# A macaron transformer block on one core: the mix stage's low-part subtractions in pieces of 256 columns, and a second factor of 1.0 in the bias scaling

## The chip, the cores and the metric

One core of one Trainium2 chip. The metric is device time in microseconds of one execution of the whole program; the kernel before takes 1156.02 us (median of 3 runs, 1155.96 to 1157.16).

## What is computed

The input `x` has 512 positions of 1024 features, in float32. One layer does, in this order:

```python
h = h + 0.5 * swiglu(rmsnorm(h, ffn1_norm), ffn1_w_gu, ffn1_w_down)      # 1024 -> 2 x 2816 -> 1024
u = rmsnorm(h, mix_norm)
qa, ka, va, qb, kb, vb, qi, ki, wi, g = split(u @ w_in)                  # 8 + 8 heads of 64, 4 index heads, 2 x 1024 gates
out_a = dsa_attention(...)     # per query the 128 keys with the best index scores
out_b = moba_attention(...)    # causal; own block of 256 and the block before
mixed = sigmoid(g_a) * (out_a @ w_branch_dsa) + sigmoid(g_b) * (out_b @ w_branch_moba)
h = h + mixed @ w_out
h = h + 0.5 * swiglu(rmsnorm(h, ffn2_norm), ffn2_w_gu, ffn2_w_down)
```

Both attentions add to their logits a bias looked up from the distance of query and key (`rel_bias`, 32 buckets, one column a head).

## The kernel before, in words

**Split products.** The matmuls take a reduced format (float32r). So that the result keeps float32's precision, every matrix is split into a high part (rounded to that format) and a low part (what rounding left), and a product is three matmuls: high by high, high by low, low by high. These are lines 118, 119 and 120, and they are most of what TensorE does.

**A weight unit.** Weights arrive in units of 128 x 1024 (some of 128 x 768 or 128 x 512) that serve one output tile. `wunit` (line 111) starts the DMA of a unit into `raw` (3 buffers) from SyncE's queue; `wsplit` (line 107) has ScalarE write the high part `whi` (line 108) and GpSimd the low part, `wlo = raw - whi` (line 109), with 3 buffers each. Ten units, late in the mix stage, and the first ones of the program have VectorE as the subtracting engine in place of GpSimd.

**Stages.** The first feed-forward block (`ffn`) takes until 380 us, the mix stage from there to 795 us, the second feed-forward block the rest. The mix stage first projects q, k and v of one head pair; then `weave` runs the MoBA attention (some 400 to 540 us) and fills TensorE's order with further projections, one step of three matmuls at a time; then come the branch products of MoBA, interleaved with gates, while VectorE finds the top 128 scores (540 to 600 us: `topk`, lines 530 to 534); then the DSA attention, woven in the same way (600 to 722 us); then the DSA branch and the output projection (to 795 us).

**One attention step.** For head and query block `i`, `logits(i)` puts the scores in PSUM (lines 587, 588), `addend(i + 1)` scales the next bias rows by the reciprocal of the query's norm, and line 596 (VectorE) adds the two and takes the row minimum; ScalarE exponentiates (line 75); `turn` transposes the probabilities on TensorE (line 623), and lines 631 and 632 split them into high and low. The scaling of the bias (`addend`, line 573) is GpSimd's in all 32 steps of MoBA and, in DSA, for the first query block of each head (40 instructions in all); the other DSA steps have it on VectorE together with the selection mask (line 570). GpSimd also multiplies each head pair's result by its reciprocal sums (line 652). The norms of q and k are small VectorE steps (lines 411 to 418, on 128 x 8) and some of 512 columns (445, 446, 453).

**Order.** TensorE's order is the program's, written by hand. The other engines' orders are set when the program is built, by a planner that plays the program through with its own costs for each instruction, and takes what is ready by priority (program order, with lines 596 and 75 of the attention raised). Each engine then runs its instructions strictly in that order.

Of the kernel before, what the change touches and what calls it, by code (L numbers as in the profile page):

```python
# [14 lines left out]
ALU = mybir.AluOpType  # L15
# [30 lines left out]
def f32(ap):  # L46
    return ap.bitcast(F32)
# [3 lines left out]
def block_kernel(ctx, tc, x, gains, wgu1, wd1, w_in, w_v, wb_a, wb_b, w_out, wgu2, wd2, rel_bias, onehot, out):  # L51
    nc = tc.nc
# [34 lines left out]
    def T(tag, bufs, shape=(P, S), dt=F32, p=sb):  # L87
        uid[0] += 1
        return p.tile(list(shape), dt, tag=tag, name=f"{tag}{uid[0]}", bufs=bufs)
# [4 lines left out]
    def mmps():  # L94
        return T("mm", 3, p=ps)
# [8 lines left out]
    def wtiles(n):  # L104
        return (T(t, b, (P, 1024), dt)[:, 0:n] for t, b, dt in (("raw", RAWS, F32), ("whi", 3, F32R), ("wlo", 3, F32R)))

    def wsplit(raw, hi, lo, eng=nc.gpsimd):
        nc.scalar.activation(hi, raw, AF.Copy)  # L108
        eng.tensor_sub(lo, raw, f32(hi))  # L109

    def wunit(src, eng=nc.gpsimd):
        raw, hi, lo = wtiles(src.shape[1])
        nc.sync.dma_start(raw, src)
        wsplit(raw, hi, lo, eng)
        return tuple(a.rearrange("p (k c) -> p k c", c=P) for a in (hi, lo))
# [10 lines left out]
    def together(gens):  # L126

        for _ in zip(*gens):
            pass
        for g in gens:  # L130
            run(g)

    def mmk(pt, w, xs):
        wh, wl = w
        n = wh.shape[1]
        for k in range(n):
            mm3(pt, wh[:, k, :], wl[:, k, :], xs[k][0], xs[k][1], k == 0, k == n - 1)
            yield
# [81 lines left out]
    def norm_r(ssum):  # L220
        p, ones = tps(), tmp()[:, 0:P]
        nc.gpsimd.memset(ones, 1.0 / D)
        nc.tensor.matmul(p, ones, ssum, start=True, stop=True)
        y, b = rsqrt_parts(p)
        r = T("R", 1)
        nc.vector.tensor_scalar(y, y, -0.5, None, op0=ALU.mult)
        nc.vector.scalar_tensor_tensor(r, b, -3.0, y, op0=ALU.add, op1=ALU.mult)
        return r
# [50 lines left out]
    def lead1(tiles, start, begun):  # L279

        ws = []
        for k in range(KD):
            nc.sync.dma_start(h[k], x[k * P:(k + 1) * P, :])
            if k % 2 == 0:
                pieces = [a.rearrange("p (k u c) -> p k u c", k=2, c=P) for a in wtiles(1024)]
            raw, hi, lo = (a[:, k % 2] for a in pieces)
            for i in range(2):
                nc.sync.dma_start(raw[:, 2 * i:2 * i + 2],
                                  wgu1[i * NF:i * NF + 2, :, k * P:(k + 1) * P].rearrange("u p c -> p u c"))
            ws.append((raw, hi, lo))  # L290
        pts = [f() for f in (mmps, mmps, sps, sps)]
        for k, (raw, hi, lo) in enumerate(ws):
            wsplit(raw, hi, lo, nc.vector)
            xs1.append(scaled(k, G_N1, h[k]))
            squares(k, ss1)
            if k == KD - 1:
                r = norm_r(ss1)
            for u, pt in enumerate(pts):
                mm3(pt, hi[:, u], lo[:, u], *xs1[k], k == 0, k == KD - 1)
        for u in (0, 2, 1, 3):  # L300
            tiles.append((pts[u], ()))
        begun[0] = 2
        start()
        return r
# [154 lines left out]
    def v_units(br, j, dsts, bank=mmps):  # L459


        vs = []

        def post(t, p):
            for e, v in enumerate(vs):
                src = p[:, e * P:(e + 1) * P].rearrange("p (e d) -> p e d", e=2)
                nc.scalar.activation(v[:, t, :, 0, :], src, AF.Copy, scale=r2T[:, t:t + 1])
                nc.vector.scalar_tensor_tensor(v[:, t, :, 1, :], src, r2T[:, t:t + 1], f32(v)[:, t, :, 0, :],
                                               op0=ALU.mult, op1=ALU.subtract)

        ws = [wunit(w_v[4 * br + 2 * j + i]) for i in range(2)]
        wh, wl = ([a.rearrange("p k c -> p (k c)").rearrange("p (k c) -> p k c", k=4)[:, k] for a in w for k in range(4)]
                  for w in zip(*ws))
        for t in range(NQ):
            if t % 2 == 0:
                p = bank()
            o = p[:, (t % 2) * 256:(t % 2 + 1) * 256]
            b = slice(t * P, (t + 1) * P)
            for k in range(KD):
                mm3(o, us[k][0][:, b], us[k][1][:, b], wh[k], wl[k], k == 0, k == KD - 1)  # L480
                if k % 2:
                    tick()
                    yield
            if t == 1:
                vs.extend(T("v", 3, (P, NQ, 2, 2, DH), F32R) for _ in dsts)
                for v, dst in zip(vs, dsts):
                    dst.append(v.rearrange("p t e s d -> p t e (s d)"))
            if t % 2:
                post(t - 1, p[:, 0:256])
                post(t, o)  # L490
# [58 lines left out]
    def attention(br, pairs, outs, extra):  # L549

        sel = br == 0
        bias, prob, tms, osum, tot, inv_s = {}, {}, {}, {}, {}, {}
# [5 lines left out]
        def rows(qt):  # L558
            return T(f"l{qt}", 1, (P, P * (qt + 1)))

        def addend(i):

            if i < 32:
                hd, qt = divmod(i, 4)
                W = P * (qt + 1)
                inv = pairs[hd // 2][0][2][:, 2 * qt + hd % 2:2 * qt + hd % 2 + 1]
                tms[i] = rows(qt)
                b = bias[hd][:, S - W:S]
                if sel and qt:
                    nc.vector.scalar_tensor_tensor(tms[i], b, inv, work[:, WOFF[qt]:WOFF[qt] + W],  # L570
                                                   op0=ALU.mult, op1=ALU.add)
                else:
                    nc.gpsimd.tensor_scalar(tms[i], b, inv, None, op0=ALU.mult)

        def logits(i):
            if i >= 32:
                return
            hd, qt = divmod(i, 4)
            if qt == 1:
                table(hd + 1)  # L580
            e = hd % 2
            (q, f, _), (k, kl), _ = pairs[hd // 2]
            W = P * (qt + 1)
            N = max(W, 256)
            p = sps()
            qb = q[:, e, qt * P:(qt + 1) * P]
            nc.tensor.matmul(p[:, 0:N], qb, k[:, e, 0:N], start=True, stop=False)
            nc.tensor.matmul(p[:, 0:N], qb, kl[:, e, 0:N], start=False, stop=True)
            addend(i + 1)
            pe = tms.pop(i)  # L590
            st = T("st", 8, (P, 4))
            if i % 8 == 0:
                tot[hd // 2] = T("tot", 2, (P, 8))
            s1 = tot[hd // 2][:, i % 8:i % 8 + 1]
            with tc.high_priority(HURRY):
                sums[i] = nc.vector.tensor_tensor_reduce(  # L596
                    out=pe, in0=p[:, 0:W], in1=pe, scale=f[:, 2 * qt + e:2 * qt + e + 1], scalar=3e38, op0=ALU.add, op1=ALU.min, accum_out=st[:, 0:1])
                log_exp(pe, pe, AF.Exp, bias=st[:, 0:1], scale=-1.0, accum_out=s1)
            prob[i] = pe
# [54 lines left out]

        table(0)
        addend(0)
        logits(0)
        yield 2
# [60 lines left out]
    def vv(br, j, **kw):  # L719
        return v_units(br, j, [a[2] for a in (dsa, moba)[br][2 * j:2 * j + 2]], **kw)  # L720

    ps3 = [mmps() for _ in range(2)]
    together([mmk(p, wunit(w_in[U_QB + 4 * i]), us) for i, p in enumerate(ps3)])
    v0 = vv(1, 0, bank=sps)
# [81 lines left out]
        run(unit(w_out[c], mixed, lambda p: wout_post(c, p)))  # L806


    def lead2(tiles, start, begun):
        start()  # L810
        together([t[1] for t in tiles])
        start()
        next(tiles[2][1])
        return norm_r(ss3)

    def emit(c, b):
        nc.sync.dma_start(out[c * P:(c + 1) * P, b], h[c][:, b])

    ffn(xs2, wgu2, wd2, emit, lead2, halves)


# [48 lines left out]
```

## Time and profile before

| | |
|---|---|
| median of 3 runs | 1156.02 us |
| profiled execution, its own time | 1157.22 us |
| its span, first to last instruction | 1155.4 us |
| granted TensorE clock, mean | 0.997 |
| TensorE busy (matmul) | 1137.6 us, 98% |
| VectorE busy | 670.6 us, 58% |
| ScalarE busy | 468.5 us, 41% |
| GpSimd busy | 529.5 us, 46% |

An engine's idle time ahead of an instruction is put down to what ended it. [...]

### The profile page before, as it was taken

To read this page: it belongs to the slowest core of one execution; us is meant where nothing else is said; L and a number is where in the kernel's file an instruction comes from. 1 tells how busy PE (TensorE), PEld (TensorE's weight loads), DVE (VectorE), ACT (ScalarE), POOL (GpSimd) and SP (SyncE) were. 2 spreads that over 40 slices of the span, in tenths; PEclk is the share of its full clock that TensorE was granted. 3 is DMA by queue.
4 is the path that set the end of the run, shared out by engine and by line. 5 is a ranking of instruction groups with operands and counts; after the bars stand their busy time and mean duration, and the time that the engine had idled before them with its cause. 6 is when DMAs were issued, how large, how long until landed. Compare 5 with 4: busy or idle time off the path is not lost.

```text
span 1155.4 us, 14050 instructions
## 1 busy us (share of the span) xinstructions
PE 1137.6 (98%) x5364; PEld 947.0 (82%) x5364; DVE 670.6 (58%) x966; ACT 468.5 (41%) x765; POOL 529.5 (46%) x283
## 2 busy tenths in 40 slices
PE   9999999999999999989999999999999999999998
PEld 7778888888888888779878877888888888888887
DVE  5864156613657468799967795764764156523551
ACT  6322123212234568758237766444322222322321
POOL 3444444444444656755454532044454444444442
PEclk9999999999999999989999999999999999999999
DMA  7233222332223221221242221322223322322322
GB/s 235 85 117 98 91 104 97 91 99 102 87 83 122 69 106 65 101 74 46 92 137 84 92 84 45 128 94 91 108 91 95 106 92 91 109 92 91 105 79 91
DMA packets 39580, 111.72 MB, mean 97 GB/s; under 512 B 4535, under 2 KB 9049, under 8 KB 39513
## 3 DMA queue, kind: packets, MB, share of 16 engines
q1 hardware_dynamic: 39368, 110.80, 29.0%
q8 instruction: 42, 0.69, 0.2%
q14 instruction: 26, 0.20, 0.1%
q10 hardware_dynamic: 144, 0.02, 0.0%
HBM read 108.64 MB, written 2.17 MB: 96 GB/s over the span
## 4 chain that ended last, share of the span: by engine, by line
PE 84%; DVE 7%; issue 4%; ACT 3%; POOL 1%; DMA 0%; SPq 0%; ACTq 0%; POOLq 0%; DVEq 0%
PE mm L120 20%; PE mm L118 20%; PE mm L119 20%; PE s L118 7%; PE s L119 7%; PE s L120 7%; DVE l L596 1%; POOL wlo L109 1%; ACT l L75 1%; PE pt L623 1%; DVE l L570 1%; DVE pt L632 1%; DVE a L146 1%; DVE fq L416 1%; POOL os L652 1%
## 5 line engine op out<-in xcount | busy, mean ns | idle before, releaser
L109 POOL TENSOR_TENSOR wlo<-raw,whi 128x1024 fp32r<-128x1024 f32 (+2 forms) x189 | 453.0, 2399 | 538.8 <-ACT whi L108 534.6
L108 ACT ACTIVATE whi<-raw 128x1024 fp32r<-128x1024 f32 (+2 forms) x207 | 205.1, 993 | 513.8 <-PE mm L119 299.0
L118 PE MATMUL mm<-x,whi 128*128 128x512 f32 x632 | 252.7, 400 | 0.5 <-ACT whi L108 0.5
L120 PE MATMUL mm<-x,wlo 128*128 128x512 f32 x632 | 247.4, 391 | 0.0
L119 PE MATMUL mm<-x,whi 128*128 128x512 f32 x632 | 247.0, 391 | 0.0
L118 PE MATMUL mm<-a,whi 128*128 128x512 f32 (+1 forms) x462 | 178.6, 387 | 1.3 <-DVE tmp L701 1.3
L120 PE MATMUL mm<-a,wlo 128*128 128x512 f32 (+1 forms) x462 | 178.6, 387 | 0.7 <-POOL wlo L109 0.7
L119 PE MATMUL mm<-a,whi 128*128 128x512 f32 (+1 forms) x462 | 178.7, 387 | 0.3
L120 PEld LDWEIGHTS mm<-x,wlo 128*128 128x128 f32 x632 | 118.9, 188 | 25.9 <-DVE wlo L109 0.3
L118 PEld LDWEIGHTS mm<-x,whi 128*128 128x128 f32 x632 | 119.4, 189 | 22.9 <-ACT whi L108 1.3
L118 PE MATMUL s<-x,whi 128*128 128x512 f32 x352 | 137.0, 389 | 0.6 <-ACT tmp L75 0.6
L120 PE MATMUL s<-x,wlo 128*128 128x512 f32 x352 | 137.0, 389 | 0.0
L119 PE MATMUL s<-x,whi 128*128 128x512 f32 x352 | 136.9, 389 | 0.0
L119 PEld LDWEIGHTS mm<-x,whi 128*128 128x128 f32 x632 | 119.2, 189 | 21.1 <-issue 0.5
L271 DVE SCALAR_TENSOR_TENSOR h<-mm,h 128x512 f32<-128x512 f32 (+1 forms) x49 | 33.3, 680 | 165.3 <-PE mm L120 165.3
L262 DVE TENSOR_TENSOR tmp<-tmp,tmp 128x512 f32<-128x512 f32 x44 | 99.0, 2250 | 29.3 <-ACT tmp L75 29.1
L146 DVE TENSOR_TENSOR a<-tmp,a 128x512 fp32r<-128x512 f32 x49 | 88.5, 1806 | 28.6 <-ACT a L145 28.3
L118 PEld LDWEIGHTS mm<-a,whi 128*128 128x128 f32 x462 | 86.8, 188 | 19.3 <-issue 1.7
L119 PEld LDWEIGHTS mm<-a,whi 128*128 128x128 f32 x462 | 86.8, 188 | 18.7 <-DVE a L146 1.1
L120 PEld LDWEIGHTS mm<-a,wlo 128*128 128x128 f32 x462 | 86.8, 188 | 18.6 <-POOL wlo L109 1.1
L118 PEld LDWEIGHTS s<-x,whi 128*128 128x128 f32 x352 | 66.1, 188 | 14.7 <-ACT tmp L75 1.0
L119 PEld LDWEIGHTS s<-x,whi 128*128 128x128 f32 x352 | 66.1, 188 | 13.8
(172 smaller groups left out, 1387.5 us busy)
## 6 DMA issues: line engine op xcount, KB each, us to landing
raw<-in_ffn_w_gu_dram SPq DMA_DIRECT2D x84, 512.0 KB, 3.4
raw<-in_w_in_dram SPq DMA_DIRECT2D x35, 512.0 KB, 3.5
raw<-in_ffn_w_down_dram SPq DMA_DIRECT2D x32, 512.0 KB, 3.5
raw<-in_ffn_w_down_dram SPq DMA_DIRECT2D x16, 384.0 KB, 3.1
bias<-fd SPq DMA_DIRECT2D x16, 256.0 KB, 3.5
raw<-in_w_v_dram SPq DMA_DIRECT2D x8, 512.0 KB, 3.4
raw<-in_w_out_dram SPq DMA_DIRECT2D x8, 512.0 KB, 3.5
h<-in_x_dram SPq DMA_DIRECT2D x8, 256.0 KB, 4.7
```

The lines of the kernel that those rows point to most:

```text
L75: op = after([group["load"]], lambda: nc.scalar.activation(*a, **k))
L108: nc.scalar.activation(hi, raw, AF.Copy)
L109: eng.tensor_sub(lo, raw, f32(hi))
L118: nc.tensor.matmul(pt, wh, xh, start=start, stop=False)
L119: nc.tensor.matmul(pt, wh, xl, start=False, stop=False)
L120: nc.tensor.matmul(pt, wl, xh, start=False, stop=stop)
L146: nc.vector.tensor_sub(lo, src, f32(hi))
L262: nc.vector.tensor_mul(g1, g1, s)
L271: nc.vector.scalar_tensor_tensor(h[c][:, b], pd, 0.5, h[c][:, b], op0=ALU.mult, op1=ALU.add)
L416: nc.vector.scalar_tensor_tensor(b, b, -3.0, y, op0=ALU.add, op1=ALU.mult)
L570: nc.vector.scalar_tensor_tensor(tms[i], b, inv, work[:, WOFF[qt]:WOFF[qt] + W], op0=ALU.mult, op1=ALU.add)
L596: sums[i] = nc.vector.tensor_tensor_reduce(out=pe, in0=p[:, 0:W], in1=pe, scale=f[:, 2 * qt + e:2 * qt + e + 1], scalar=3e38, op0=ALU.add, ...
```

## The change

`wsplit` gets a piece width. It is 1024 at first, so one instruction a unit as before; it is set to 256 ahead of the first projections of the mix stage and back to 1024 ahead of the second feed-forward block. In between, each subtraction on GpSimd goes in pieces of 256 columns: four for a unit of 1024 columns, two for one of 512. Subtractions on VectorE, and tiles of more than two dimensions, stay whole. In `addend`, GpSimd's multiplication of the bias by a per-row factor gets a second multiplication, by 1.0.

```diff
+    piece = [1024]
+
     def wsplit(raw, hi, lo, eng=nc.gpsimd):
         nc.scalar.activation(hi, raw, AF.Copy)
-        eng.tensor_sub(lo, raw, f32(hi))
+        if len(raw.shape) > 2 or eng is not nc.gpsimd:
+            eng.tensor_sub(lo, raw, f32(hi))
+            return
+        for c in range(0, raw.shape[1], piece[0]):
+            b = slice(c, min(c + piece[0], raw.shape[1]))
+            eng.tensor_sub(lo[:, b], raw[:, b], f32(hi)[:, b])
...
-                    nc.gpsimd.tensor_scalar(tms[i], b, inv, None, op0=ALU.mult)
+                    nc.gpsimd.tensor_scalar(tms[i], b, inv, 1.0, op0=ALU.mult, op1=ALU.mult)
...
+    piece[0] = 256
     ps3 = [mmps() for _ in range(2)]
...
+    piece[0] = 1024
     def lead2(tiles, start, begun):
```

## Rows read from the trace of the kernel before

**Rows 1.** The page's first part: busy us, share of the span, instructions.
```profile
PE 1137.6 (98%) x5364; PEld 947.0 (82%) x5364; DVE 670.6 (58%) x966; ACT 468.5 (41%) x765; POOL 529.5 (46%) x283
```

**Rows 2.** Stretches: length, busy PE, PEld, DVE, ACT, POOL (instructions), PEclk, DMA.
```profile
400.00:540.00 140.00, 134.90 (x747) 115.11 (x746) 113.53 (x260) 97.22 (x209) 88.41 (x60) 0.98 0.25 86
540.00:600.00 60.00, 57.98 (x273) 48.01 (x273) 55.38 (x117) 23.46 (x36) 27.59 (x17) 1.00 0.27 92
600.00:722.00 122.00, 117.19 (x645) 99.35 (x645) 88.86 (x192) 82.22 (x182) 51.22 (x30) 1.00 0.25 81
```

**Rows 3.** Waits of TensorE, 362 to 795 us: total us, times, longest.
```profile
PE s L587 <- DVE st L596: 4.2, 2, 3.1
PE pt L623 <- DVE pt L632: 3.7, 4, 1.7
PE mm L118 <- DVE tmp L701: 1.3, 1, 1.3
PE pt L623 <- ACT rw L611: 0.8, 1, 0.8
PE mm L120 <- POOL wlo L109: 0.7, 1, 0.7
```

**Rows 4.** Timeline of VectorE: start, us, line, operation, out<-in.
```profile
400.71 2.78 DVE L446 TENSOR_TENSOR tmp<-tmp,tmp 128x512 f32<-128x512 f32 x1
...
434.47 2.37 DVE L415 TENSOR_TENSOR fq<-fq 128x8 f32<-128x8 f32 x1
...
482.85 2.08 DVE L517 TENSOR_SCALAR work<-tmp,wtok 128x512 f32<-128x512 f32 x1
...
493.60 2.37 DVE L416 SCALAR_TENSOR_TENSOR fq<-fq 128x8 f32<-128x8 f32 x1
...
562.85 2.46 DVE L534 TENSOR_SCALAR work<-work 128x384 f32<-128x384 f32 x1
...
592.79 0.42 DVE L534 TENSOR_SCALAR work<-work 128x512 f32<-128x512 f32 x1
...
618.32 2.38 DVE L416 SCALAR_TENSOR_TENSOR fq<-fq 128x8 f32<-128x8 f32 x1
```

**Rows 5.** Timeline of GpSimd at the same places.
```profile
397.73 8.03 POOL L109 TENSOR_TENSOR wlo<-raw,whi 128x1024 fp32r<-128x1024 f32 x3
...
434.02 2.79 POOL L109 TENSOR_TENSOR wlo<-raw,whi 128x1024 fp32r<-128x1024 f32 x1 [1.17 <-ACT whi L108]
...
482.27 2.38 POOL L109 TENSOR_TENSOR wlo<-raw,whi 128x1024 fp32r<-128x1024 f32 x1
...
493.07 2.87 POOL L109 TENSOR_TENSOR wlo<-raw,whi 128x1024 fp32r<-128x1024 f32 x1 [2.17 <-DVE fq L415]
...
642.84 4.98 POOL L109 TENSOR_TENSOR wlo<-raw,whi 128x1024 fp32r<-128x1024 f32 x2 [2.55 <-ACT whi L108]
647.78 1.60 POOL L652 TENSOR_TENSOR os<-os,rb 128x512 f32<-128x512 f32 x1
```

**Rows 6.** Line 109's instructions: ns min/median/max, first and last start.
```profile
L109 POOL TENSOR_TENSOR wlo<-raw,whi x189: 1287/2393/3017, 19.6 to 1140.6; 128x1024 fp32r<-128x1024 f32 x165, 128x768 fp32r<-128x768 f32 x16, 128x512 fp32r<-128x512 f32 x8
```

**Rows 7.** GpSimd by line and shape, 362 to 795 us: busy, mean ns, idle before.
```profile
L109 POOL TENSOR_TENSOR wlo<-raw,whi 128x1024 fp32r<-128x1024 f32 x52 | 128.6, 2480 | 134.6 <-ACT whi L108 130.4 <-DVE fq L415 2.2 <-issue 1.6
L573 POOL TENSOR_SCALAR l<-bias,fq 128x512 f32<-128x512 f32 x8 | 13.3, 1657 | 2.4 <-PE pt L623 2.4
L573 POOL TENSOR_SCALAR l<-bias,fq 128x128 f32<-128x128 f32 x16 | 11.3, 704 | 38.7 <-DVE fq L418 12.3 <-PE pt L623 10.7 <-ACT k L452 10.0
...
L109 POOL TENSOR_TENSOR wlo<-raw,whi 128x512 fp32r<-128x512 f32 x8 | 10.5, 1321 | 19.8 <-ACT whi L108 19.8
...
L522 POOL TENSOR_SCALAR_AFFINE_SELECT work<-work 128x128 f32<-128x128 f32 x3 | 0.9, 294 | 1.4 <-DVE work L519 1.4
```

**Rows 8.** Line 109 alone in a stretch: length, POOL busy, PEclk, DMA.
```profile
400.00:540.00 140.00, 42.58 (x18) 0.98 0.25 86
```

**Rows 9.** Stretch behind TensorE's longest wait, columns as in Rows 2.
```profile
499.00:504.50 5.50, 5.46 (x14) 4.38 (x15) 5.45 (x15) 3.50 (x8) 1.50 (x2) 0.50 0.16 47
```

## The prediction

> **What bounds the kernel now.** I read the page's first part, then the busy times by stretch, then TensorE's waits in the mix stage, then the two timelines at the places of those waits. TensorE is busy 98% of the span [rows 1]; no other engine comes near, so only time in which TensorE stands still or runs at its lower clock can be won. The change touches only the mix stage. There TensorE is idle 140 - 134.90 = 5.1 us, 60 - 57.98 = 2.0 us and 122 - 117.19 = 4.8 us in the three stretches of [rows 2], 11.9 us in all. The waits name who ended them [rows 3]: VectorE's 4.2 + 3.7 + 1.3 = 9.2 us, ScalarE 0.8, GpSimd's low parts 0.7; the reader is to see that GpSimd itself is hardly ever what TensorE waits for.
>
> So what makes VectorE late? The timeline has line 415, on 128 x 8, at 2.37 us [rows 4]. An instruction on eight columns can't need that. It starts 0.45 us after GpSimd began a unit's subtraction at 434.02 [rows 5] and ends at 436.84, where that one ends (436.81). Line 416 at 493.60 ends at 495.97, GpSimd's unit at 495.94; line 517 at 482.85 ends at 484.93, the unit at 484.65. Line 534 takes 2.46 us at 562.85 and 0.42 us, on more columns, at 592.79 [rows 4]. A VectorE instruction of these kinds that meets a running GpSimd subtraction stands until it has ended, and then does its own work.
>
> Between two GpSimd instructions VectorE gets in. Three units run back to back from 397.73 in 8.03 us, where three alone would be 3 x 2.39 = 7.2 [rows 5, 6]; line 446 starts at 400.71 within them and ends 2.78 us later [rows 4]. It did not have to wait for all three, and the units lost 0.8 us, this one and another visit together.
>
> TensorE's longest wait, 3.1 us, ends with line 596 [rows 3] behind lines 517 and 416 on VectorE's queue. Behind it the granted clock is 0.50, the lower of its two levels, for the 5.5 us to 504.5 [rows 9]: TensorE had stood still before the fall, and work of 2.75 us at the upper level took 5.5. That is 2.75 us more to win; shorter waits (1.7 us and less) left the clock at 1.00 in their stretches [rows 2, 3].
>
> **The change, part by part.**
>
> *A piece's cost.* 512 columns take 1.287 us undisturbed, 1024 take 2.393 [rows 6]: 2.16 ns a column and 0.18 us an instruction. A piece of 256 is then 0.735 us, four are 2.94 us (0.54 more a unit), two are 1.47 (0.18 more). By the code 35 units of `w_in`, 8 of `w_v` and 6 of `w_out` are cut in four, the 8 of MoBA's branch in two; of the 52 in [rows 7] the last three belong to the second feed-forward block. GpSimd gets 49 x 0.54 + 8 x 0.18 = 28 us of work more, in 49 x 3 + 8 = 155 more instructions. Where it is densest, from 400 to 540 us, 18 units [rows 8] add 9.7 us to 88.4 of 140 [rows 2]: 98 of 140. It stays off the bound, so this work costs nothing by itself; it costs where GpSimd's own result is next.
>
> *Shorter blocks.* A blocked VectorE instruction now waits for a piece, 0.735 us at the most. Going through TensorE's waits: line 415 at 434.47 is released at 434.76 in place of 436.81, 2 us earlier, more than the wait of 4.2 - 3.1 = 1.1 us at its end: 1.1 back. Line 517 is released 1.5 us earlier and line 416 at 493.60 two: 3.5 us on a queue that runs without a pause to line 596; of the 3.1 us I take 2.6, as line 445 there still stands behind line 652, which is not cut. With a stall that short the low clock should go: I take 2.3 of 2.75. Line 701's 1.3 us come from a full VectorE (55.4 of 60 us busy [rows 2]); line 534 alone, 2.0 us too long, covers them: 1.3. Of the 3.7 us for line 632 the longest, 1.7, lies behind line 416 at 618.32: 1.5 back; two of the other three have the same cause, 1.0 back. For its low part TensorE waits 0.7; the first piece is there 0.55 us earlier, if a matmul waits only for the piece it reads: 0.5. Sum: 1.1 + 2.6 + 2.3 + 1.3 + 1.5 + 1.0 + 0.5 = 10.3 us.
>
> *Longer GpSimd.* Line 652, the pair's scaling, stands behind two units at 642.84 [rows 5]; its result goes through ScalarE and VectorE to one of TensorE's four waits for line 632 [rows 3]. The two units are 1.1 us longer now, so this wait grows by 1.1; the wait of 0.8 on ScalarE [rows 3] has one unit in its chain and grows by 0.5. If the planner puts line 652 between pieces, both shrink instead, the first by its size, (3.7 - 1.7) / 3 = 0.7 at the mean, the second by 0.5: 1.2 back. I take the loss, -1.6.
>
> *The neutral factor.* 40 instructions. No row has the form with two operations. The one-operation form takes 1657 ns for 512 columns and 704 for 128, disturbances included; the nearest other one-input operation on GpSimd, line 522, takes 294 ns for 128 [rows 7]. Low end: all 40 at half their time, 21 us off GpSimd, but nothing in [rows 3] waits for them, so at most another 0.3 us of shorter blocks. High end: a second pass over the columns. The slope is (1657 - 704) / 384 = 2.5 ns a column, the 40 have 11,264 columns, 28 us more, nearly all before 540 us. I take no change, the row of the same instruction.
>
> [...]
>
> *Given back.* TensorE's order is fixed, so a wait removed lets it arrive earlier at the next, and many instructions finish just in time. The planner, too, sees other costs and orders the queues anew. I take -1.0.
>
> 10.3 - 1.6 - 1.0 = 7.7 us. From the profiled execution: 1157.2 - 7.7 = 1149.5; it lies 1.2 us over the median, so 1148.3, rounded to 1148.
>
> **The rivals.**
>
> *More comes back, 1144 us.* Line 652 slips between pieces, the neutral factor is cheaper, nothing is given back: 10.3 + 1.2 + 0.3 = 11.8 us, from 1156. For it: what ends nearly all waits is a blocked VectorE. Against: it takes the planner's luck at every place.
>
> *Given back later, 1155 us.* VectorE's blocks shrink, but the waits pass to the chain line 596, ScalarE's exponential, line 631, line 632, which is near its limit (from 400 to 540 us VectorE has 113.5 and ScalarE 97.2 of 140 us [rows 2]), or a new order of the queues makes new waits. Then only the wait of 3.1 us becomes shorter, by some 1 us: within 0.2% (2.3 us, what a measurement of this kernel can tell from no change).
>
> *GpSimd becomes the bound, 1161 us, slower.* Place: MoBA's attention. It decides when GpSimd's work there reaches 140 us. 98 come from above. If at each of the 18 x 3 new borders a VectorE instruction takes its turn for some 0.4 us (half of the 0.8 lost at 397.73), that is 22 more, 120; with the second pass of 28 us, 148. Then that stretch grows by 8 us over 140, and bias rows come late to line 596. The 3 us won outside (1.3 + 1.5 + 1.0 + 0.5 - 1.6) leave 1156 + 8 - 3 = 1161. Against: it takes the high end of an unseen cost and a visitor at every border.
>
> *The pieces hold the port together, 1160 us, slower.* If a queued piece follows so closely that VectorE never gets in, a block lasts for the whole unit, now 0.54 us longer; the seven blocks on TensorE's path named above (415, 517, 416 twice, 534 and two more) cost 3.8 us. Line 446 [rows 4, 5] speaks against it. [...]
>
> **How the numbers follow.** Forecast 0.58; more 0.14; given back 0.15; GpSimd the bound 0.08; port held 0.05. The forecast's own range is 1145 to 1152. The range goes from 1143, which leaves out a third of the case of more, 0.05, to 1157, past the case of no change, which leaves out the slower ones, 0.13. Faster by over 0.2%: 0.58 + 0.14 = 0.72; within: 0.15; slower: 0.13.
>
> **What would show it.** Line 109 in the mix stage with some 0.73 us a piece, 155 more of them; lines 415 and 416 never over about 0.9 us there except behind line 652; TensorE's waits on lines 596 and 632 at some 2 to 3 us in place of 7.9; no stretch of clock 0.50 around 500 us; feed-forward stages as before. Wrong, if line 573 gets much longer, if small VectorE instructions still take over 2 us, or if the idle time stays and only its releasers change names, to lines 109 and 652.

## The result and the profile after

The changed kernel takes 1146.41 us (median of 4 runs, 1146.27 to 1146.44) against 1155.99 beside it: a ratio of 0.9917, 95% interval 0.9902 to 0.9931, 9.6 us less. The profiled execution took 1146.42 us with a span of 1144.6, against 1155.4. Its mean clock is 1.0.

In the kernel after, lines stand a little lower: 109 is 117, 415 to 417 are 423 to 425, 446 is 454, 517 is 525, 573 is 581, 587 is 595, 596 is 604, 611 is 619, 623 is 631, 632 is 640, 652 is 660. The experiments further down keep the numbers of before.

In the rows PE is TensorE, PEld its weight loads, DVE VectorE, ACT ScalarE and POOL GpSimd; the clock is the granted TensorE clock as a share of its upper level, and 0.50 and 1.00 are the two levels seen in the traces of before and after.

The page's first part (busy us, share of the span, instructions) has GpSimd with 155 instructions more, as worked out, and VectorE with 24.9 us less of busy time than in [rows 1]: time in which it had only stood.

```profile
PE 1133.0 (99%) x5364; PEld 946.0 (83%) x5364; DVE 645.7 (56%) x966; ACT 468.0 (41%) x765; POOL 545.4 (48%) x438
```

The busy times by stretch (length, then PE, PEld, DVE, ACT, POOL, the clock, DMA), against [rows 2, 9]. The last line is the stretch behind the former long wait, which now comes some 4 us earlier.

```profile
400.00:540.00 140.00, 136.95 (x790) 118.57 (x789) 110.77 (x271) 101.70 (x217) 83.00 (x110) 1.00 0.26 84
540.00:600.00 60.00, 60.00 (x267) 49.70 (x267) 47.55 (x107) 20.66 (x30) 36.89 (x50) 1.00 0.33 110
600.00:722.00 122.00, 119.24 (x656) 101.53 (x655) 87.02 (x200) 85.61 (x186) 50.21 (x63) 1.00 0.24 79
...
495.00:500.50 5.50, 4.87 (x25) 3.94 (x26) 5.46 (x15) 3.70 (x9) 2.16 (x4) 1.00 0.44 143
```

TensorE's idle time in the three stretches is 3.05 + 0 + 2.76 = 5.8 us in place of 11.9; since the kernel runs ahead, the same window holds somewhat more work. The middle stretch has none left, and the clock near 500 stays at 1.00.

TensorE's waits, 362 to 790 us (total, times, longest), against [rows 3]:

```profile
PE pt L631 <- DVE pt L640: 3.0, 4, 1.7
PE s L595 <- DVE st L604: 1.5, 2, 0.9
PE pt L416 <- ACT rw L619: 0.7, 1, 0.7
PE pt L631 <- ACT rw L619: 0.3, 1, 0.3
```

The two that were 7.9 us are 4.5. The waits for line 701 and for the low part no longer appear. The longest, 1.7, is one that was 0.8 before; it is the subject of a step below.

VectorE's timeline (start, us, line, operation): the instructions of [rows 4], the one ahead of the first, and, from 434 to 438, what follows one of them:

```profile
399.99 0.95 DVE L453 SCALAR_TENSOR_TENSOR tmp<-tmp,tmp 128x512 f32<-128x512 f32 x1
400.98 1.11 DVE L454 TENSOR_TENSOR tmp<-tmp,tmp 128x512 f32<-128x512 f32 x1
...
434.40 0.70 DVE L423 TENSOR_TENSOR fq<-fq 128x8 f32<-128x8 f32 x1
435.03 1.04 DVE L527 SCALAR_TENSOR_TENSOR work<-tmp,wtok,work 128x256 f32<-128x256 f32 x1
435.99 0.70 DVE L424 SCALAR_TENSOR_TENSOR fq<-fq 128x8 f32<-128x8 f32 x1
...
437.29 1.30 DVE L461 SCALAR_TENSOR_TENSOR low<-tmp,gqk,k 64x512 fp32r<-64x512 f32 x1
...
481.18 0.88 DVE L525 TENSOR_SCALAR work<-tmp,wtok 128x512 f32<-128x512 f32 x1
...
491.10 0.15 DVE L424 SCALAR_TENSOR_TENSOR fq<-fq 128x8 f32<-128x8 f32 x1
...
557.46 0.35 DVE L542 TENSOR_SCALAR work<-work 128x384 f32<-128x384 f32 x1
...
610.25 0.70 DVE L424 SCALAR_TENSOR_TENSOR fq<-fq 128x8 f32<-128x8 f32 x1
```

What took 2.37 us takes 0.70, or 0.15 where no piece was running. Between 380 and 770 us, 36 VectorE instructions began while a piece ran and lasted at least 0.1 us longer than the shortest of their kind in these traces. Of these 34 got in behind the piece they met; lines 527 (435.03) and 578 (611.58) began 0.05 us before a piece's end and let the next one pass as well. The longest by its row is 1.30 us, its own work included.

GpSimd's timeline at the places of [rows 5] (an x3 or x8 is that many instructions back to back):

```profile
395.47 6.07 POOL L117 TENSOR_TENSOR wlo<-raw,whi 128x256 fp32r<-128x256 f32 x8
...
433.96 2.71 POOL L117 TENSOR_TENSOR wlo<-raw,whi 128x256 fp32r<-128x256 f32 x3 [1.83 <-ACT whi L111]
436.65 0.69 POOL L581 TENSOR_SCALAR l<-bias,fq 128x512 f32<-128x512 f32 x1
437.31 0.74 POOL L117 TENSOR_TENSOR wlo<-raw,whi 128x256 fp32r<-128x256 f32 x1
...
633.37 6.14 POOL L117 TENSOR_TENSOR wlo<-raw,whi 128x256 fp32r<-128x256 f32 x8 [2.79 <-ACT whi L111]
639.48 1.29 POOL L660 TENSOR_TENSOR os<-os,rb 128x512 f32<-128x512 f32 x1
```

A piece alone is 0.74 us; eight with VectorE's visits are 6.14 where two whole units were 4.98. Line 581 shows the surprise: 0.69 us for 512 columns, where [rows 7] have a mean of 1.66. GpSimd by shape, 362 to 790 us (busy, mean ns, idle before), answers to [rows 7]:

```profile
L117 POOL TENSOR_TENSOR wlo<-raw,whi 128x256 fp32r<-128x256 f32 x212 | 168.6, 825 | 128.6 <-ACT whi L111 123.4 <-DVE a L154 2.2 <-issue 1.7
...
L581 POOL TENSOR_SCALAR l<-bias,fq 128x128 f32<-128x128 f32 x16 | 6.7, 418 | 35.5 <-DVE fq L426 11.9 <-ACT k L460 9.6 <-PE pt L631 7.8
...
L581 POOL TENSOR_SCALAR l<-bias,fq 128x512 f32<-128x512 f32 x8 | 6.0, 755 | 2.9 <-PE pt L631 2.9
```

Where did the 10.8 us of span come from? On TensorE, VectorE and ScalarE the sequence of instructions is the same in both kernels, and so is that of GpSimd's other 94 instructions; but seven of these now stand between the pieces of a unit, where they stood behind it (line 581 at 436.65 is one). In the trace no other engine's idle time ends on any of the seven. So the same TensorE instruction can be looked up in both traces, and each jump in the difference of its two starts is a gain or a loss at that place. The steps over 0.25 us (times are those of the kernel before, from its first instruction; at 383 to 387 a gain and a loss of 0.5 cancel, and are left out):

```
at us       what TensorE waited for there            step, us   predicted
439         line 596, behind 415                      -0.5       -1.1
473-476     line 632 and others, behind 519           -1.2        0
495-499     line 596, behind 517 and 416              -2.3       -2.6
499-504     clock 0.50 -> 1.00                        -1.8       -2.3
534         given back, in a short wait               +0.5       +1.0
590         line 701                                  -1.6       -1.3
594         low part                                  -1.1       -0.5
625-628     line 632, behind 416                      -1.4       -1.5
652         line 632, behind 652                      +0.9       +1.1
666, 679    line 632                                  -1.1       -1.0
686, 704    short waits                               -0.7        0
713         ScalarE, line 611                         -0.4       +0.5
sum                                                  -10.7       -7.7
```

The clock's row is what was left of 2.4 us: the matmuls themselves gained that much, and 0.6 of it went into a new wait for line 632.

### The profile page after: what moved, and what is told of

Its sections match the earlier page's. It is cut to its first block, busy times and chain, and to the rows that moved or that the text cites. A ratio compares the mean times of both kernels' runs of the same rounds, so it can differ in the third digit from the quotient of the medians.

```text
span 1144.6 us, 14239 instructions
## 1 busy us (share of the span) xinstructions
PE 1133.0 (99%) x5364; PEld 946.0 (83%) x5364; DVE 645.7 (56%) x966; ACT 468.0 (41%) x765; POOL 545.4 (48%) x438
## 4 chain that ended last, share of the span: by engine, by line
PE 91%; DVE 5%; ACT 2%; issue 1%; POOL 1%; DMA 0%; SPq 0%; ACTq 0%; DVEq 0%; POOLq 0%
PE mm L126 21%; PE mm L127 21%; PE mm L128 21%; PE s L126 7%; PE s L128 7%; PE s L127 7%; PE pt L631 1%; DVE l L604 1%; PE s L595 1%; PE s L596 1%; POOL wlo L117 1%; PE o L650 1%; PE o L651 1%; PE pt L416 1%; DVE a L154 0%
## 5 line engine op out<-in xcount | busy, mean ns | idle before, releaser
L117 POOL TENSOR_TENSOR wlo<-raw,whi 128x256 fp32r<-128x256 f32 (+2 forms) x344 | 489.8, 1442 | 520.9 <-ACT whi L111 515.8
L270 DVE TENSOR_TENSOR tmp<-tmp,tmp 128x512 f32<-128x512 f32 x44 | 99.0, 2249 | 29.3 <-ACT tmp L75 29.1
L154 DVE TENSOR_TENSOR a<-tmp,a 128x512 fp32r<-128x512 f32 x49 | 89.5, 1829 | 28.5 <-ACT a L153 28.3
L126 PEld LDWEIGHTS s<-x,whi 128*128 128x128 f32 x352 | 66.0, 188 | 14.6 <-ACT tmp L75 1.0
L128 PEld LDWEIGHTS s<-x,wlo 128*128 128x128 f32 x352 | 66.2, 188 | 13.7
```

What stands on the lines that cost most here:

```text
L117: eng.tensor_sub(lo[:, b], raw[:, b], f32(hi)[:, b])
L126: nc.tensor.matmul(pt, wh, xh, start=start, stop=False)
L128: nc.tensor.matmul(pt, wl, xh, start=False, stop=stop)
L154: nc.vector.tensor_sub(lo, src, f32(hi))
L270: nc.vector.tensor_mul(g1, g1, s)
```

## The experiments

The theories, with the letters that the expectations use: A, shorter pieces let VectorE in sooner and the rest follows; B, the second factor makes the bias scaling cheaper and that is a good part of the gain; C, TensorE gains since the first piece of a low part is ready early; D, GpSimd's pieces hold VectorE out together. Each ran beside the kernel before (its medians 1156.07 to 1156.3 in the three sets). The pieces are the same three lines in all of them, with the width set ahead of the mix stage and back to 1024 behind it:

```diff
-    uid = [0]
+    uid, piece = [0], [1024]
...
+    cut = lambda eng, *ts: zip(*([t[:, c:min(c + piece[0], t.shape[1])] for c in range(0, t.shape[1], piece[0])] if eng is nc.gpsimd else [t] for t in ts))
...
-        eng.tensor_sub(lo, raw, f32(hi))
+        [eng.tensor_sub(*abc) for abc in cut(eng, lo, raw, f32(hi))]
```

**Pieces of 256 alone**, no second factor.

```diff
-    ps3 = [mmps() for _ in range(2)]
+    piece[0], ps3 = 256, [mmps() for _ in range(2)]
```

> Pieces of 256 columns in the mix stage, bias scaling with one factor as before. Theory A (what made TensorE wait was VectorE standing behind whole-unit subtractions on GpSimd, and the pieces shorten that): nearly the whole gain is here, 1147 to 1148.5 us against 1156.0, lines 415 and 416 never over 0.9 us except behind line 652, no stretch of clock 0.50 near 500 us. Rival B (the second factor did it, since the bias scaling of 512 columns went from 1.57 to 0.69 us with it and so freed some 20 us of GpSimd): less than half of the gain, 1152 us or more, and VectorE still late behind line 573.

Measured: 1146.21 us (1145.96 to 1146.35), ratio 0.9913 [0.9899, 0.9926]. The pieces alone bring the whole gain.

**The second factor alone**, whole units.

```diff
-                    nc.gpsimd.tensor_scalar(tms[i], b, inv, None, op0=ALU.mult)
+                    nc.gpsimd.tensor_scalar(tms[i], b, inv, 1.0, op0=ALU.mult, op1=ALU.mult)
```

> Whole-unit subtractions as before, bias scaling with the second factor 1.0 alone. Theory A: TensorE waited for no bias row before, so 1155 to 1156 us; line 573 at 0.69 us for 512 columns, lines 415 and 416 still at 2.37 us. Rival B: 1151 us or less.

Measured: 1152.9 us (1152.46 to 1153.82), ratio 0.9972 [0.9961, 0.9982]: neither number. The factor alone is worth 3.2 us, though the pieces leave it nothing to give (1146.41 with it, 1146.21 without). GpSimd is busy for 509.4 us in place of 529.5. All of the gain arises between 472 and 504 us; in the timelines of this kernel, VectorE's first, then GpSimd's, one sees how:

```profile
482.17 0.48 DVE L517 TENSOR_SCALAR work<-tmp,wtok 128x512 f32<-128x512 f32 x1
...
492.36 2.36 DVE L417 SCALAR_TENSOR_TENSOR fq<-fq,r2q 128x8 f32<-128x8 f32 x1
```

```profile
479.95 2.41 POOL L109 TENSOR_TENSOR wlo<-raw,whi 128x1024 fp32r<-128x1024 f32 x1
...
492.25 2.45 POOL L109 TENSOR_TENSOR wlo<-raw,whi 128x1024 fp32r<-128x1024 f32 x1 [2.18 <-ACT whi L108]
```

Behind shorter bias scalings GpSimd starts a unit at 479.95, not 482.27 [rows 5]. It has 0.2 us left when line 517 comes, which takes 0.48 us, not 2.08 [rows 4]. One of the two blocks ahead of the long wait is gone by a shift in time, the other is still there (line 417 in place of 416). Behind the shorter wait the clock stayed up. Waits of TensorE, and the stretch of [rows 9]:

```profile
PE s L587 <- DVE st L596: 2.5, 2, 1.5
```

```profile
499.00:504.50 5.50, 5.50 (x31) 4.72 (x30) 5.43 (x19) 4.03 (x10) 3.28 (x3) 1.00 0.02 7
```

The longest wait is 1.5 us and not 3.1, and the clock is 1.00.

**Pieces of 512, 171 and 128**, each with the second factor: the dose.

```diff
-    piece[0] = 256
-    ps3 = [mmps() for _ in range(2)]
+    piece[0], ps3 = 512, [mmps() for _ in range(2)]     # and 171, and 128
```

> Both parts, with pieces of 512 columns (units of 512 whole). Theory A: a block lasts up to 1.29 us in place of 0.74 (whole units 2.39), so roughly two thirds of the gain: 1149 to 1151 us, the longest wait near 495 us about 1.5 us. Rival C (the gain comes from the first piece of a unit being ready early, and from other GpSimd work slipping between pieces): the first piece comes 1.1 us after the start in place of 1.66 us sooner; also a part of the gain, but the small VectorE steps would be no measure of it.

> Both parts, with pieces of 171 columns (six a unit, three for the units of 512): 0.55 us a piece by 0.18 us + 2.16 ns a column. With 128 columns VectorE's line 445 was held at 399.86 through 14 pieces (6.2 us), with 256 never through more than one. Theory D1 (below some length of a piece a VectorE instruction doesn't get in between two): either 171 is above that length, no block passes over more than one or two pieces, and the time is 1145.5 to 1148; or it is below, a block of several us shows again, and the time is 1150 or more. Theory D2 (the 14 pieces were the worse for more work alone): 1148 to 1150, no block over 1.3 us.

> Both parts, with pieces of 128 columns. A piece is 0.46 us by the line through the shapes seen (0.18 us and 2.16 ns a column), a unit 3.65 us, 1.26 us more than whole. Theory A: blocks are 0.28 us shorter still than with 256, but GpSimd has some 36 us more work than with 256 and line 652 stands behind longer units: 1145 to 1148 us, near the kernel with 256. If GpSimd's length weighs more than the blocks, 1148 to 1150.

```
columns   us, median (lowest to highest)     ratio to before
1024      1152.9  (1152.46 to 1153.82)       0.9972 [0.9961, 0.9982]
 512      1147.86 (1147.36 to 1149.51)       0.9932 [0.9919, 0.9944]
 256      1146.41 (1146.27 to 1146.44)       0.9917 [0.9902, 0.9931]
 171      1146.25 (1146.09 to 1147.87)       0.9918 [0.9904, 0.9931]
 128      1154.44 (1152.87 to 1156.28)       0.9985 [0.9977, 0.9994]
```

Half the length already brings most of the gain, more than the expectation had (1149 to 1151); 171 columns bring no more than 256; and at 128 nearly all of it is lost, which neither number of that expectation had. Down to 256 the order of the times is A's; the last line is what D says. VectorE's and GpSimd's timelines with 128 columns:

```profile
399.86 6.16 DVE L445 SCALAR_TENSOR_TENSOR tmp<-tmp,tmp 128x512 f32<-128x512 f32 x1
```

```profile
395.35 10.12 POOL L109 TENSOR_TENSOR wlo<-raw,whi 128x128 fp32r<-128x128 f32 x24
```

24 pieces run back to back, 0.42 us apart, and line 445, with 0.69 us of work of its own, stands for 5.5 us, until the last of them has ended (405.47). Behind it TensorE gets a wait that no kernel with longer pieces has, and then the low clock (waits, and a stretch):

```profile
PE pt L378 <- ACT tmp L370: 3.4, 1, 3.4
```

```profile
410.50:416.00 5.50, 5.50 (x16) 4.42 (x17) 3.79 (x6) 3.46 (x5) 3.17 (x6) 0.50 0.00 0
```

By the same comparison of starts this place costs 6.2 us, and the loss at 652 is 2.0 in place of 0.9, while the gains at 495 to 499, 590, 594 and 625 are still there. With 171 columns the same instruction, and the burst beside it:

```profile
399.80 2.41 DVE L445 SCALAR_TENSOR_TENSOR tmp<-tmp,tmp 128x512 f32<-128x512 f32 x1
```

```profile
395.47 6.20 POOL L109 TENSOR_TENSOR wlo<-raw,whi 128x171 fp32r<-128x171 f32 x12
```

That is 1.7 us of standing, four ends of pieces 0.52 us apart, and again until the burst is over (401.67). The time fits the first case of that expectation, the hold does not. Such holds are few: counted as for the kernel after, nine of 40 held instructions let two or more pieces pass with 171 columns, and twelve of 40 with 128, most of them by beginning within 0.1 us of a piece's end. Only line 445 at 400 us and, with 128 columns, line 519 at 480 (2.79 us) stood through more than two.

**Pieces of 128 without the factor**, one execution: does a burst of short pieces hold VectorE out by itself, or did the shifted start of GpSimd's work do it?

```diff
-    ps3 = [mmps() for _ in range(2)]
+    piece[0], ps3 = 128, [mmps() for _ in range(2)]
```

> Pieces of 128 columns without the second factor: the look at 128 columns once more, with the bias scaling at its old length. D1: line 445 (or its neighbours) near 400 us is again held through many pieces, 5 to 6 us. D2: the hold was one execution's, and no block is over 1.5 us here.

Measured: 1157.15 us, span 1155.4, clock 0.997. VectorE's and GpSimd's timelines:

```profile
399.92 8.41 DVE L445 SCALAR_TENSOR_TENSOR tmp<-tmp,tmp 128x512 f32<-128x512 f32 x1
```

```profile
397.68 10.11 POOL L109 TENSOR_TENSOR wlo<-raw,whi 128x128 fp32r<-128x128 f32 x24
```

Line 445 now stands until the last piece of the burst has ended (407.79), 7.7 us. So the hold needs no second factor; what GpSimd did before the pieces only moves the burst.

**Pieces of 256 in reverse order**, with the factor: the same blocks, but the piece that TensorE reads first comes last.

```diff
-        [eng.tensor_sub(*abc) for abc in cut(eng, lo, raw, f32(hi))]
+        [eng.tensor_sub(*abc) for abc in list(cut(eng, lo, raw, f32(hi)))[::-1]]
```

> Both parts, pieces of 256 columns, but written from the last columns of a unit to the first, so that the columns that TensorE reads first come last. Theory A (shorter blocks of VectorE): the blocks are as short as with the change, only the 1.0 us won at the wait for a low part (594 us) and 0.5 us near 383 us may go: 1146.5 to 1148 us. Rival C (first pieces early): most of the gain goes, 1151 us or more.

Measured: 1147.6 us (1147.16 to 1148.27), ratio 0.9926 [0.9914, 0.9939]. The order is worth about 1 us of the 9.6; C is not the cause. TensorE's waits show the part that it is, at 383 us:

```profile
PE s L119 <- POOL wlo L109: 0.9, 1, 0.9
```

Against the kernel after, the starts lose 1.0 us there, of which 0.6 comes back by 387, and 0.3 more at the low part of 594.

**Pieces of 256 in the feed-forward stages too**, with the factor.

```diff
-    uid, piece = [0], [1024]
+    uid, piece = [0], [256]
...
-    piece[0] = 1024
```

> Both parts, with pieces of 256 columns in the feed-forward stages too (139 more units in pieces). Theory A, with the reading that a block costs only where TensorE waits behind it: VectorE's busy time falls by about 60 to 90 us there (lines 146 and 262 at 0.7 to 1.3 us in place of 1.8 and 2.25), and the time stays within 1 us of the change's 1146.4, since TensorE is idle for under 3 us before 362 us. If short blocks are worth something by themselves: 1144 us or less. If longer GpSimd work counts: over 1148.

Measured: 1145.59 us (1144.3 to 1147.09), ratio 0.9911 [0.9896, 0.9926]. The groups of VectorE's two lines that stand most (busy, mean ns, idle before):

```profile
L146 DVE TENSOR_TENSOR a<-tmp,a 128x512 fp32r<-128x512 f32 x49 | 54.0, 1104 | 28.4 <-ACT a L145 28.3
L262 DVE TENSOR_TENSOR tmp<-tmp,tmp 128x512 f32<-128x512 f32 x44 | 36.4, 827 | 32.5 <-ACT tmp L75 32.3
```

In the kernel after they take 1829 and 2249 ns. VectorE is busy for 542.2 us in place of 645.7, a hundred us less, and the span is 1.6 us shorter; the two intervals overlap. Blocks cost time where TensorE waits for what stands in them, and in the feed-forward stages it hardly does: before 362 us it is idle for 2.1 us in the kernel after.

This kernel also has line 445 standing through a burst of pieces of 256 columns:

```profile
398.74 1.67 DVE L445 SCALAR_TENSOR_TENSOR tmp<-tmp,tmp 128x512 f32<-128x512 f32 x1
```

```profile
394.23 5.63 POOL L109 TENSOR_TENSOR wlo<-raw,whi 128x256 fp32r<-128x256 f32 x8
```

It meets a piece with 0.42 us left, lets the next and last one pass too, and is done 0.55 us behind the burst's end (399.86). The last kernel below has the same. In the kernel after, the same line (453 there) met such a burst at 399.99 (eight pieces from 395.47) and got in behind the first piece. So at 256 columns too VectorE does not always get in between two pieces; here it cost 1.0 us.

**Which form of the bias scaling is the cheap one**, one execution, whole units: heads take turns between one factor, a second factor 1.0, an added 0.0, and 1.0 again.

```diff
-                    nc.gpsimd.tensor_scalar(tms[i], b, inv, None, op0=ALU.mult)
+                    nc.gpsimd.tensor_scalar(tms[i], b, inv, *((None, ALU.mult), (1.0, ALU.mult, ALU.mult), (0.0, ALU.mult, ALU.add), (1.0, ALU.mult, ALU.mult))[hd % 4])
```

> Whole-unit subtractions; the bias scaling in three forms by head: one factor (heads 0 and 4 of each attention), a second factor 1.0 (heads 1, 3, 5, 7), a second operation that adds 0.0 (heads 2 and 6). If any second operation brings the fast form, 512 columns take 0.69 us in the last two and 1.56 in the first; if only two multiplications do, adding 0.0 takes 1.56 us or more.

GpSimd's timeline; the first line is head 0's 256, 384 and 512 columns in one row, then head 2 (an added 0.0) and head 3 (times 1.0) with 512, and head 4, one factor again, with 384:

```profile
394.20 3.71 POOL L573 TENSOR_SCALAR l<-bias,fq 128x256 f32<-128x256 f32 x3
...
450.53 0.69 POOL L573 TENSOR_SCALAR l<-bias,fq 128x512 f32<-128x512 f32 x1 [3.34 <-PE pt L623]
...
466.83 0.70 POOL L573 TENSOR_SCALAR l<-bias,fq 128x512 f32<-128x512 f32 x1
...
478.20 1.24 POOL L573 TENSOR_SCALAR l<-bias,fq 128x384 f32<-128x384 f32 x1
```

Both second operations gave the short form, 0.69 and 0.70 us for 512 columns; between these two, what it computes made no difference. The kernel took 1155.32 us.

**Line 652 first**: a higher priority for the pair's scaling, which lost 0.9 us behind the longer units.

```diff
-                eng.tensor_mul(osum[0], osum[0], inv_s.pop(hd // 2))
+                with tc.high_priority(HURRY): eng.tensor_mul(osum[0], osum[0], inv_s.pop(hd // 2))
```

> Both parts, and the scaling of a head pair's result (line 652) raised in the planner's priority, so that it can go ahead of pieces that are ready. The change lost 0.9 us at TensorE's wait near 652 us, where line 652 stands behind two units. If the planner moves it: that wait of 1.7 us shrinks by 1 to 1.5 us and the time is 1144.5 to 1146. If not, or if the pieces behind it become late: 1146.4 or more.

Measured: 1146.28 us, ratio 0.9915 [0.9901, 0.9928]. The planner left the line where it was, so this says nothing of its cost.

**Line 652 on VectorE** in the stage where it waits, with pieces and factor; then the same with pieces in all stages.

```diff
-                eng = nc.vector if sel and hd == 7 else nc.gpsimd
+                eng = nc.vector if sel else nc.gpsimd
```

> Both parts, with line 652 on VectorE for all four head pairs of the DSA attention (only the last before). If the wait at 644 us of the changed kernel (1.7 us) is line 652 behind two units on GpSimd: its result comes some 3 us earlier, the wait goes, and with it part of the waits near 669 and 703 us: 1144.0 to 1145.5 us against 1146.4. If VectorE's own queue is the limit there: 1146.4 or more.

Measured: 1144.27 us (1144.2 to 1146.06), ratio 0.9898 [0.9885, 0.9912]. TensorE's waits, with the 1.7 of the kernel after gone:

```profile
PE s L587 <- DVE st L596: 1.5, 2, 0.9
PE pt L623 <- DVE pt L632: 1.5, 3, 0.6
```

In the comparison of starts the step at 652 is -1.8 against the kernel after: the loss there and the old wait both went. The intervals of the two ratios overlap, and the order on VectorE is another here; the step at that place is the evidence. (The profiled execution is the slowest of the four and had lost 1.4 us within its first 10 us.)

> Pieces of 256 columns in all stages, both parts, and line 652 on VectorE in the DSA attention. If the gains of the single steps add (0.8 us from the feed-forward stages, 1 to 2 from line 652): 1143 to 1144.5 us, the fastest so far. If they overlap: 1144.5 to 1146.

Measured: 1143.17 us (1142.43 to 1144.49), ratio 0.9886 [0.9873, 0.9900], the best version here, 13.1 us under the kernel before beside it by the medians; about 3.2 of these lie beyond the change that was asked about.

## Why the prediction held, step by step

**The mechanism** was right: VectorE's long instructions of [rows 4] stood until the running subtraction on GpSimd had ended, 2.37 and 2.38 us for eight columns beside whole units (2.39 alone), and the same lines took 0.15 to 0.70 among pieces of 0.74; what mattered is how long that subtraction is. The pieces alone bring the gain, the dose from 1024 to 256 columns orders the times as it should, and no new order on TensorE, VectorE or ScalarE can stand behind it, for there is none. On GpSimd seven instructions moved up between pieces, and nothing on another engine waited for them. The traces show how long VectorE stood and beside what, and not what in the hardware holds it. The sign that missed was the waits on lines 596 and 632: 4.5 us in place of the 2 to 3 named. Of these 0.65 is left at 439, 0.9 at 495 and 0.6 is new behind it, where the sum had 0, 0.5 and 0.

**A piece's cost**, 0.735 us: measured 0.721 to 0.740 undisturbed and 0.825 at the mean. In the mix stage they came to 168.6 us where the units had taken 131.9 ([rows 7], less the 7.2 of the last three): 37 more, where 28 were worked out without VectorE's visits. GpSimd as a whole was 83.0 of 140 from 400 to 540 us, not 98, since the bias scaling went the other way.

**Line 596 at 439**: 0.4 of 1.1 came back at the wait itself (0.5 in the table, with small steps before it). The block on line 415 shrank as foreseen, but the rows from 434.40 on show what the step left out. Before, one whole unit was let pass, and what followed on the queue ran almost free. In the trace of before these were:

```profile
436.76 0.48 DVE L519 SCALAR_TENSOR_TENSOR work<-tmp,wtok,work 128x256 f32<-128x256 f32 x1
437.17 0.57 DVE L416 SCALAR_TENSOR_TENSOR fq<-fq 128x8 f32<-128x8 f32 x1
...
438.34 0.73 DVE L453 SCALAR_TENSOR_TENSOR low<-tmp,gqk,k 64x512 fp32r<-64x512 f32 x1
```

Now the three meet a piece of their own: line 527 takes 1.04 us where 519 took 0.48, line 424 0.70 where 416 took 0.57, and line 461 1.30 where 453 took 0.73. That gives back 0.56 + 0.13 + 0.57 = 1.3 us of the 1.7 won on line 415, which leaves the 0.4.

**The long wait and the clock**: 2.3 and 1.8 us for 2.6 and 2.3. The wait of 3.1 us became one of 0.9. The clock by itself gave 2.4 of the 2.75 us; 0.6 of this was handed on to line 632's wait at once. The granted clock, 0.50 for 5.5 us behind the 3.1 us [rows 9] and again behind the 3.4 us with 128 columns, stayed at 1.00 behind every wait of 1.7 us and less that the trace of before has from 362 to 795 us, all through the kernel after, where the longest is 1.7, and behind waits of 2.2 us with 171 columns and 2.8 with 128 (at 643 and 650; 1.0 is the mean of the execution with 171, 1.00 that of 600 to 722 us with 128).

**Lines 701, 632 and the low part**: 1.6, 2.5 and 1.1 us for 1.3, 2.5 and 0.5. That a matmul waits only for the piece it reads fits the reversed kernel at 383: line 119 waits 0.9 us for the low part there, and in the kernel after the trace has no such wait. Of the low part's 1.1 us at 594 only 0.3 hangs on it; for the rest, GpSimd starts that unit 1.8 us ahead of TensorE's matmul (584.70 for 586.53), not 0.8, since line 701 and with it ScalarE's work ahead of the unit come earlier. The sum counted the two as separate.

**Longer GpSimd**: at 652 the loss was 0.9 for 1.1, by the foreseen chain: two units and line 652 took 4.98 + 1.60 us [rows 5] and take 6.14 + 1.29, 0.85 more, and TensorE's wait there went from 0.8 to 1.7. Moving line 652 to VectorE removed it. At 713 the sign was wrong, a gain of 0.4 for a loss of 0.5; no run isolates why.

**The neutral factor** is the step that failed. It was taken as no change, with at most 0.3 us if it halved the instruction. It halves it, 42.1 us for the 40 instructions before and 21.3 after: undisturbed, 128 columns take 367 ns and 512 take 688 with the second factor, 597 and about 1560 without, so 0.84 ns a column against 2.5. The bound of 0.3 us failed too, for it looked at who waits for the bias and not at when the following unit starts: alone, the factor is worth 3.2 us. Why the form with one operation takes three times as long a column, no run shows. The sum came out close since the pieces had already taken the blocks that the factor would have moved.

**Not foreseen**: 1.2 us at 473 to 476, behind line 519, which stood for 2.85 us at 467.94 before, and 0.7 us of short waits. **Given back**: 1.0 was taken, 0.5 came. In sum 10.7 us came where 7.7 were forecast: 1.9 from the places not foreseen, 0.9 from 713, 0.6 from the low part, 0.5 not given back, less 0.6 at 439 and 0.5 for the clock, and small ones. That single terms missed both ways by half a microsecond and more, and the total lay inside the range, is in part luck. The medians differ by 1.2 less than the spans, as the profiled execution of before lay that much over its median and that of after did not.

**The rivals**: GpSimd was nowhere near the bound. That pieces keep VectorE out together was false at 256 columns in the kernel after, and true for line 445 at 128. The prediction's word for what they hold, a port, is its author's assumption; no run shows it. That the pieces' length bears on it, the prediction couldn't see from whole units. What decides is open. In five of the traces here line 445 stood until the burst beside it had ended: 1.0 us with 256 columns (in the two kernels with pieces in all stages), 1.7 with 171, 5.5 and 7.7 with 128. In the kernel after it got in behind one piece of 256, and most held instructions got in so at every length. The length of a piece is therefore not the whole reason; how much of a burst was left when the instruction came set how long it stood. No run varies the gap between two pieces apart from their length, so none shows whether that gap decides it.

## What to carry to other kernels

Look for small VectorE instructions with a duration far over that of their columns, and see what GpSimd runs beside them; here it was 2.37 us on eight columns beside a unit of 2.39. Cutting the GpSimd instruction helped where TensorE waited behind such a block: 1156.07 us became 1146.21 with the pieces alone. Do not cut it finer than the gain asks for: 171 columns brought no more than 256, and at 128 one VectorE instruction that stood through a whole burst took nearly all of the gain. Look for such a hold in the trace at every length. Work out the gain along the whole queue, for later instructions can pay for a piece again: at 439 us they gave back 1.3 of 1.7. An engine that nobody waits for can still decide, by when it starts, which of its neighbours are blocked: with the second factor alone a unit began at 479.95 in place of 482.27, and line 517 took 0.48 us in place of 2.08.

## What was not expected of the hardware

GpSimd's multiplication of a tile by a per-row factor was slower with one operation (1.56 us for 512 columns) than with a second, neutral one (0.69). Short GpSimd instructions in a burst kept a VectorE instruction, line 445, out until the burst ended, for as much as 7.7 us with pieces of 128 columns, over three times the 2.39 us of a whole unit, though they followed each other at 0.42 us.
